# GpSimd's large work in the attention stage moves to VectorE and ScalarE

## The chip, the cores and the metric

The kernel runs on one core of one Trainium2 chip. The metric is device microseconds of one execution. The engines are TensorE (PE: matmuls and transposes; its weight loads are PEld), VectorE (DVE), ScalarE (ACT), GpSimd (POOL), and the DMA queue that SyncE (SP) issues.

## The reference

One step of a hybrid encoder layer, D_MODEL = 1024, 1024 new frames (prompt) and 32 frames of a running stream (sample, with 512 cached frames), 16 heads of 64. Both branches read one normed input `h`:

```python
q, k  = rmsnorm per head of h @ w_q, h @ w_k;  v = h @ w_v
logf  = log_sigmoid(h @ w_f + b_f)                 # forget gates, c = cumsum(logf)
u     = (h @ w_ua) * sigmoid(h @ w_ub)
s     = q k^T + c[t] - c[s], causal;  o = softmax(s) v
conv  = causal depthwise conv of u, width 31, + b_dw
ya    = (o * silu(h @ w_ga)) @ w_pa
yb    = (silu(layernorm(conv)) * silu(h @ w_gb)) @ w_pb
y     = x + (sigmoid(h @ w_ma) * ya + sigmoid(h @ w_mb) * yb) @ w_out
```

k, v, logf and the last 30 rows of u are outputs too, for both streams.

## The kernel before

All large products run on TensorE as three 16-bit products (high x high, high x low, low x high), so every operand is split into a high half (a rounded copy, on ScalarE) and a low half (value less high half, on VectorE or GpSimd). Weights come in blocks of 128 output columns. A `Batch` of two blocks loads them, takes their sum of squares on ScalarE (`stage`), totals it on PE (`total`), forms a power of two (`power`), and splits (`high`, `low`).

A projection of one block is 24 *beats*; a beat is three matmuls. `beat()` is the clock of the program's order: at each beat it runs what is due (`later(n, fn)` means n beats on) and, by a rate that each stage sets, takes instructions from `taps`. The order so made is kept for PE, VectorE, ScalarE (and SP in the attention stage).

`taps` is the list of VectorE's convolution steps. Per block f of 128 channels, `conv_taps(f)` appends 50 items: 46 multiply-adds of 128 x 543 (lines 402, 407, 411), 3 additions or subtractions (420 to 423), and a first item on ScalarE. `sums(f)` gives two more items for the LayerNorm's sums: `from_shift` (y less the mean over channels of block 0, line 359) and `into_sums` (line 366), each over pieces of 1024 and 32 columns; nine beats later ScalarE squares y, and four beats behind that GpSimd adds it into `rstd` (line 373). Block f's sums stand among the taps of block f+1; block 7's are run 28 beats after its last tap. After that `sides["ready"]` is set.

`u_tile(f)` opens the input block of a convolution; for f over 3 it first runs taps until at most 155 are left. At the end of the ga gates taps are run until at most 97 are left.

While the ga gates are projected (about 480 to 582 us), four `Sample` objects do the running stream's attention. `Sample.turn` (lines 1176 to 1182) transposes the softmax on PE in four full blocks and one of 32 rows. Both go to the one-bank PSUM pool "tr", each followed by a ScalarE copy out. The pool "st" has two banks.

The attention stage of the prompt (about 582 to 970 us) is a loop over 128 units, a unit being 128 queries of one head against 128 to 1024 keys. In each pair of heads the four query quarters come in the order 3, 1, 2, 0; a quarter holds two blocks of 128 queries, each for both heads (e = 0, 1). At step k the program issues:

- `scores` of unit k (PE, lines 1288 to 1290, into one of two banks pairs psS), `high` of unit k-3 (ScalarE, line 1318: the high half PH of P, the softmax)
- `top` and `soft` of unit k (VectorE's maximum, line 1297; ScalarE's exponential into P with its sum, line 1303)
- on even k the reciprocal of the sums, and the DMA transposes PH to PT (line 1335) of units k-5 and k-4
- what was put down for k: loads of the next pair, `values` (PE, line 1356, PT times V) eight units behind, `gated` (VectorE, line 1370)
- `low` of unit k-3, then taps as far as `slack` allows; one step of the LayerNorm generator `ln`, if `ready` is set and no bank is held.

P has four buffers and PH five; once `ready` is set, every third unit uses freed convolution tiles in place of these (`spare`). Between those steps come the *fills*: 22 blocks of the gb, ma and mb gates, 528 beats, spread over the units by the planner's cost per unit (`heavy`, `matmuls`).

`low` has two forms. For e = 0, and for all units once `taps` is empty, VectorE does it in one instruction (line 1327). For e = 1 while taps are left, GpSimd does it in two: P is scaled in place (line 1324), then PH's high half is subtracted (line 1325). The same condition governs the fill weights' high halves: while taps are left GpSimd makes them (line 154), and afterwards ScalarE (line 156). The planner's VectorE cost `vector(k)` counts `low` accordingly. The taps per unit follow from

```python
slack += R_A * (each * heavy(k) - vector(k) - 0.15 * share_of)     # R_A = 0.7
while taps and slack >= 0:
    slack -= 1.3 * (taps.pop(0)() or 1.0)                           # a tap returns 0.56, a sum nothing
```

Of the kernel before, what the change touches and what calls it, by code (L numbers as in the profile page):

```python
# [8 lines left out]
F32 = mybir.dt.float32  # L9
# [5 lines left out]
ALU = mybir.AluOpType  # L15
# [44 lines left out]
def build(tc, xT, xt, wv, wf, ckT, cv, clT, stT, vec, cst, yT, kT, vO, lfO, cpT, csT):  # L60
    nc = tc.nc
# [3 lines left out]
    def pool(name, bufs=1, stack=es, **kw):  # L65
        return stack.enter_context(tc.tile_pool(name=name, bufs=bufs, reuse_waits="tile", **kw))
# [27 lines left out]
    class Batch:  # L94
# [55 lines left out]
                                        op0=ALU.mult, op1=ALU.mult)  # L150

        def high(self, i, wh, raw, ks):
            if sides.get("cast") == "pool" and taps:
                nc.gpsimd.tensor_scalar(wh[:, ks, :], raw[:, ks, :], self.s[:, i:i + 1], 1.0, op0=ALU.mult, op1=ALU.mult)
                return
            nc.scalar.mul(wh[:, ks, :], raw[:, ks, :], self.s[:, i:i + 1])  # L156

        def low(self, i, wl, wh, raw, ks):
            nc.vector.scalar_tensor_tensor(wl[:, ks, :], raw[:, ks, :], self.s[:, i:i + 1], wh[:, ks, :],  # L159
                                           op0=ALU.mult, op1=ALU.subtract)  # L160
# [50 lines left out]
    def later(n, fn):  # L211

        pace["n"] += 1
        late.append((pace["tick"] + n, pace["n"], fn))
        late.sort(key=lambda e: e[:2])
# [89 lines left out]
    class Banks:  # L305

        n = 0
# [6 lines left out]
    st = pool("st", 2, stack=pps, space=PS)  # L314
    tr = pool("tr", 1, stack=pps, space=PS)
# [5 lines left out]
    taps = []  # L321
    pend = []

    def pump(n):
        for _ in range(min(n, len(taps))):
            taps.pop(0)()

    PCS = ((0, T, 0), (T + 30, TS, T))
    sides = {}

    def rounded(y):
        yr = cvp.tile([128, TT], F32R, name="shift", bufs=1)
        for o, n, a in PCS:
            nc.scalar.copy(yr[:, a:a + n], y[:, o:o + n])
# [17 lines left out]
    def kept(f, y):  # L352
        nc.sync.dma_start(s_y[f, :, :T], y[:, :T])
        nc.sync.dma_start(s_y[f, :, T:], y[:, T + 30:])

    def from_shift(f, y):
        shift = sides["shift"]
        for o, n, a in PCS:
            nc.vector.tensor_sub(y[:, o:o + n], y[:, o:o + n], shift[:, a:a + n])

    def into_sums(f, y):
        for o, n, a in PCS:
            if f == 0:
                nc.vector.tensor_copy(mean[:, a:a + n], y[:, o:o + n])
            else:
                nc.vector.tensor_add(mean[:, a:a + n], mean[:, a:a + n], y[:, o:o + n])

        def added():
            for o, n, a in PCS:
                if f == 0:  # L370
                    nc.gpsimd.tensor_copy(rstd[:, a:a + n], y[:, o:o + n])
                else:
                    nc.gpsimd.tensor_add(rstd[:, a:a + n], rstd[:, a:a + n], y[:, o:o + n])
            if f == 7:
                sides["ready"] = True

        later(9, lambda: nc.scalar.activation(y, y, AF.Square))
        later(13, added)

    def sums(f):  # L380
        return [lambda: from_shift(f, sides["y", f]), lambda: into_sums(f, sides["y", f])]

    def conv_taps(f):
        u = us.pop(f)

        w = lambda i: vec_t[:, V_WDW + f * KC + i:V_WDW + f * KC + i + 1]
        even, odd = u[:, 0:UW:2], u[:, 1:UW:2]
        V = nc.vector

        def ordered(t):  # L390
            if f > 5:
                tc.keep_in_program_order(t)
            return TAP

        def both(j):
            wj = wsum[:, f, j:j + 1]
            if j == 0:
                y = sides["y", f] = (u7p if f > 5 else cvp).tile([128, CW], F32, name="y", tag="y", bufs=2 if f > 5 else 3)
                nc.scalar.activation(y[:, 1:CW:2], odd[:, :CN], AF.Identity, bias=vcol(V_BDW, f), scale=wj)  # L399
                return 0.1  # L400
            y = sides["y", f][:, 1:CW:2]
            return ordered(V.scalar_tensor_tensor(y, odd[:, j:j + CN], wj, y, op0=ALU.mult, op1=ALU.add))  # L402

        def own(j):
            y = sides["y", f]
            e, o = y[:, 0:CW:2], y[:, 1:CW:2]
            return ordered(V.scalar_tensor_tensor(e, odd[:, j:j + CN], w(2 * j), e if j else o, op0=ALU.mult, op1=ALU.add))  # L407

        def other(j):
            o = sides["y", f][:, 1:CW:2]  # L410
            t = ordered(V.scalar_tensor_tensor(o, odd[:, j:j + CN], w(2 * j + 1), o, op0=ALU.mult, op1=ALU.add))  # L411
            if j == 14:
                kept(f, sides["y", f])
                if f == 7:
                    later(28, lambda: [fn() for fn in sums(7)])
            return t

        n = CN + 14
        items = [lambda j=j: both(j) for j in range(16)]
        items.append(lambda: ordered(V.tensor_sub(odd, even, odd)))  # L420
        items += [lambda j=j: own(j) for j in range(16)]
        items.append(lambda: ordered(V.tensor_sub(odd[:, :n], odd[:, :n], even[:, :n])))
        items.append(lambda: ordered(V.tensor_add(odd[:, :n], odd[:, :n], even[:, 1:1 + n])))
        items += [lambda j=j: other(j) for j in range(15)]
        if f < 6:
            taps.insert(max(0, len(taps) - 9), items.pop(0))
        if f == 7:
            taps.extend(items[:14] + pend + items[14:])
            pend.clear()
        else:  # L430
            taps.extend(items[:5] + pend + items[5:])
            pend[:] = sums(f) if f else []
# [5 lines left out]
        return ((slice(0, T - o), slice(30 + o, 30 + T)), (slice(T - o, n), slice(60 + T, 60 + T + TS)))  # L438

    def u_tile(f):  # L440
        if f > 3:
            pump(len(taps) - 155)
        u = us[f] = (u7p if f > 5 else cvp).tile([128, UW], F32, name="u", tag="u", bufs=2 if f > 5 else 4)
        nc.vector.memset(u[:, 0:30], 0.0)
        nc.sync.dma_start(u[:, 30 + T:60 + T], stT[f])
        return u
# [85 lines left out]
    def vcol(base, f):  # L532
        return vec_t[:, base + f:base + f + 1]
# [68 lines left out]
    def x_split(c, ws, u, jobs, ahead={}):  # L602
# [6 lines left out]
        def project(i, kt):  # L609
# [8 lines left out]
            if c == 2:  # L618
                for o2, n2, a2 in PCS:
                    b = slice(30 + o2, 30 + o2 + n2)  # L620
# [110 lines left out]
    for f in range(8):  # L731
# [15 lines left out]
    b2 = plan[0]  # L747
    x_split(0, ws0, u0, {
        0: [lambda: high(0, 0), lambda: low(0, 0), lambda: top(1), lambda: squares(2, False), lambda: low_pool(0, 1, True)],
        1: [lambda: squares(3), gains],  # L750
        2: [lambda: low_pool(0, 2, True), balance],
# [81 lines left out]
    for c in range(4):  # L833
# [16 lines left out]
        for t in range(8):  # L850
            ps = pj.tile([128, 512], F32, name="pjv", tag="pj")
            n = 0
            for kt in range(KT):
                sl = slice(t * 128, t * 128 + 128)
                wh, wl = wh2[kt // 4][:, kt % 4, :], wl2[kt // 4][:, kt % 4, :]
# [268 lines left out]
    class Sample:  # L1124
# [44 lines left out]
        def turn(self):  # L1169
            pf = self.pf  # L1170
            self.pts = pts = sp.tile([128, 7, 128], F32, name="pts", tag="kc", bufs=1)
            g = self.g
            nc.gpsimd.memset(pts[:, 4:7, :], 0.0)
            self.vn = pts[:, 5:7, :].rearrange("p a n -> p (a n)")
            nc.sync.dma_start(pts[:TS, 5:7, :], s_vs[:, 256 * g:256 * g + 256].rearrange("p (a n) -> p a n", a=2))
            pt = tr.tile([128, 512], F32, name="ptr2", tag="tr")
            for b in range(4):
                nc.tensor.transpose(pt[:, 128 * b:128 * b + 128], pf[:, 128 * b:128 * b + 128], ident)
            nc.scalar.copy(pts[:, 0:4, :], pt.rearrange("p (b q) -> p b q", b=4))
            pt = tr.tile([128, 512], F32, name="ptr2", tag="tr")  # L1180
            nc.tensor.transpose(pt[:TS, :128], pf[:, PAST:], ident)
            nc.scalar.copy(pts[:TS, 4, :], pt[:TS, :128])

# [59 lines left out]
    class Two:  # L1243
        n = 0
# [23 lines left out]
    class Unit:  # L1268
# [51 lines left out]
        def low(self):  # L1320
            n = self.i + 1
            f = self.f
            if self.e and taps:
                nc.gpsimd.tensor_scalar(self.P3, self.P3, f, 1.0, op0=ALU.mult, op1=ALU.mult)  # L1324
                nc.gpsimd.tensor_sub(self.H[:, :n, 1, :], self.P3, self.H[:, :n, 0, :])  # L1325
            else:
                nc.vector.scalar_tensor_tensor(self.H[:, :n, 1, :], self.P3, f, self.H[:, :n, 0, :],  # L1327
                                               op0=ALU.mult, op1=ALU.subtract)

        def turn(self):  # L1330
            i, e, m = self.i, self.e, self.i // 2
# [108 lines left out]
    width = lambda k: units[k].w if 0 <= k < len(units) else 0  # L1440
# [10 lines left out]

    def vector(k):

        return (0.31 + 0.00104 * width(k) + (0.1 + 0.001 * width(k - 3) if k % 2 or not taps else 0.0) +
                (0.5 if (k - 4 - LAG) % 4 == 0 else 0.0))

    BEAT = 0.447
# [9 lines left out]
    for g, p in enumerate(duos):  # L1467
# [9 lines left out]
        for n, m in enumerate(MORD):  # L1477
            k = t + 4 * n + 3 + LAG
# [65 lines left out]
    class Banks3:  # L1544
        n = 0
# [180 lines left out]
    parts = {}  # L1726
# [273 lines left out]
```

## Time and profile before

| | |
|---|---|
| median of 3 runs | 1252.08 us (1250.56 to 1255.34) |
| the profiled execution | 1253.4 us |
| its span, first to last instruction | 1251.5 us |
| mean granted TensorE clock | 0.995 |
| busy: PE, DVE, ACT, POOL | 1219.6, 1005.7, 791.8, 400.4 us |
| attention stage, taps present | about 582 to 724 us |
| attention stage, taps gone | about 724 to 970 us |

In the profile's windows each engine's busy time in the stretch is followed by its number of instructions, then come the granted TensorE clock, the share of DMA time and GB/s. A group's line reads: line, engine, operation, tiles written and read, shapes, count | busy us, mean ns of one | idle time before them and what ended it. A line of waits reads: who waited for whom, us in total, times, the longest. A line of the timeline reads: start, duration, engine, line, operation, and in brackets the idle time before it and what ended it.

### The profile page before, as it was taken

The page shows a single profiled execution, that of the slowest core. Times are in us where ns is not written, and L with a number is a line of the kernel's source. Part 1 is how long each engine was busy: PE and PEld are TensorE (multiplying, and loading weights), DVE is VectorE, ACT ScalarE, POOL GpSimd, SP SyncE. Part 2 cuts the span into 40 slices and gives each one's busy share as a digit, 9 for nine tenths or more (in the row PEclk, how much of TensorE's full clock was granted, in tenths as well). Part 3 has the DMA queues.
Part 4 walks back from the last instruction along what each step waited for, and adds up shares of the span by engine and source line. Part 5 has one row for each costly group of instructions (what it writes and reads, how often), then busy time and mean ns, then how long its engine had stood idle before and what let it go on. Part 6 is the DMA issues. An engine that isn't in the chain of part 4 may idle for free.

```text
span 1251.5 us, 24832 instructions
## 1 busy us (share of the span) xinstructions
PE 1219.6 (97%) x9288; PEld 852.1 (68%) x9288; DVE 1005.7 (80%) x1563; ACT 791.8 (63%) x1511; POOL 400.4 (32%) x443
## 2 busy tenths in 40 slices
PE   8999999999999999999899999999999999999998
PEld 5678786666666666666566656666666666666898
DVE  6799999988989999788999967887755586677764
ACT  5655554867768686446666777887866776644410
POOL 4046372637447271100565511000000000022652
PEclk9999999999999999999999999999999999999999
DMA  6335252332433246544999999999999885543561
GB/s 238 104 97 166 59 138 56 108 117 65 130 93 111 75 120 186 183 154 121 189 223 222 204 220 212 214 223 221 217 213 208 331 307 202 206 163 125 162 194 58
DMA packets 260840, 207.63 MB, mean 166 GB/s; under 512 B 187504, under 2 KB 223216, under 8 KB 260720
## 3 DMA queue, kind: packets, MB, share of 16 engines
q1 hardware_dynamic: 260576, 205.97, 61.1%
q8 instruction: 73, 1.20, 0.4%
q14 instruction: 47, 0.39, 0.1%
q10 hardware_dynamic: 144, 0.07, 0.0%
HBM read 110.97 MB, written 57.26 MB: 134 GB/s over the span
## 4 chain that ended last, share of the span: by engine, by line
PE 79%; DVE 6%; issue 5%; ACT 4%; POOL 4%; DMA 2%; SPq 0%; POOLq 0%; DVEq 0%; ACTq 0%
PE pj L201 56%; PE pjv L857 7%; PE pj L1830 6%; PE po L1356 3%; PE psS L1288 2%; PE psS L1289 1%; POOL PH L1325 1%; POOL P L1324 1%; DMA PT<-PH 1%; DVE y L402 1%; DVE wl L159 1%; ACT P L1303 1%; ACT PH L1318 1%; DVE nm L1297 1%; DVE PH L1327 1%
## 5 line engine op out<-in xcount | busy, mean ns | idle before, releaser
L201 PEld LDWEIGHTS <-wh 128*128 128x128 f16 x3840 | 376.0, 98 | 201.8 <-issue 2.4
L201 PE MATMUL pj<-xh,wh 128*128 128x352 f16 (+2 forms) x1536 | 481.1, 313 | 1.8 <-DVE qn L1003 1.6
L201 PE MATMUL pj<-xl,wh 128*128 128x352 f16 (+2 forms) x1536 | 480.5, 313 | 1.4 <-DVE xl L639 1.3
L201 PE MATMUL pj<-xh,wl 128*128 128x352 f16 (+2 forms) x1536 | 480.5, 313 | 0.1
L201 PEld LDWEIGHTS <-wl 128*128 128x128 f16 x1920 | 187.9, 98 | 90.5 <-issue 2.4
L159 DVE SCALAR_TENSOR_TENSOR wl<-raw,sc,wh 128x512 f16<-128x512 f32 (+1 forms) x158 | 131.9, 847 | 36.8 <-ACT wh L156 34.8
L1297 DVE TENSOR_REDUCE nm<-psS 128x1 f32<-128x1024 f32 (+7 forms) x128 | 96.4, 753 | 59.9 <-PE psS L1290 53.4
L1303 ACT ACTIVATE P<-psS,nm 128x1024 f32<-128x1024 f32 (+7 forms) x128 | 94.2, 736 | 63.5 <-DVE nm L1297 31.3
L402 DVE SCALAR_TENSOR_TENSOR y<-u,wsum,y 128x543 f32<-128x543 f32 x120 | 116.2, 968 | 4.8 <-ACT y L399 2.3
L149 POOL TENSOR_SCALAR sc<-sc,back 128x2 f32<-128x2 f32 (+1 forms) x37 | 25.9, 699 | 293.3 <-DVE sc L175 291.7
L407 DVE SCALAR_TENSOR_TENSOR y<-u,vec_t,y 128x543 f32<-128x543 f32 x128 | 115.1, 899 | 2.5
L411 DVE SCALAR_TENSOR_TENSOR y<-u,vec_t,y 128x543 f32<-128x543 f32 x120 | 108.0, 900 | 2.4
L1327 DVE SCALAR_TENSOR_TENSOR PH<-P,nm,PH 128x896 f16<-128x896 f32 (+7 forms) x106 | 91.1, 859 | 14.0 <-ACT PH L1318 12.9
L1318 ACT ACTIVATE PH<-P,nm 128x1024 f16<-128x1024 f32 (+7 forms) x128 | 98.4, 770 | 3.0 <-DMA PT<-PH 0.9
L156 ACT ACTIVATE wh<-raw,sc 128x1024 f16<-128x1024 f32 (+1 forms) x72 | 80.7, 1127 | 17.0 <-DVE sc L176 16.9
L121 ACT ACTIVATE junk<-raw 128x1024 bf16<-128x1024 f32 x78 | 81.8, 1049 | 0.2
L988 POOL TENSOR_TENSOR sql<-sqf,sqh 128x352 fp32r<-128x352 f32 x48 | 57.8, 1205 | 60.8 <-ACT sqh L985 60.7
L1288 PE MATMUL psS<-KB,QB 128*128 128x512 f16 (+2 forms) x192 | 63.3, 330 | 12.8 <-ACT P L1303 12.6
L857 PE MATMUL pjv<-vwh,xh 128*128 128x260 f16 x256 | 70.1, 274 | 0.0
L857 PE MATMUL pjv<-vwl,xh 128*128 128x260 f16 x256 | 70.0, 273 | 0.0
L857 PE MATMUL pjv<-vwh,xl 128*128 128x260 f16 x256 | 69.9, 273 | 0.0
L1356 PE MATMUL po<-PT,Vh 128*64 128x256 f16 (+1 forms) x640 | 56.3, 269 | 5.0 <-DMA PT<-PH 5.0
(318 smaller groups left out, 2372.1 us busy)
## 6 DMA issues: line engine op xcount, KB each, us to landing
raw<-wf SPq DMA_DIRECT2D x92, 512.0 KB
kT<-kun SPq DMA_DIRECT2D x8, 528.0 KB
s_ga<-t SPq DMA_DIRECT2D x24, 176.0 KB
s_gb<-t SPq DMA_DIRECT2D x24, 176.0 KB
s_ma<-t SPq DMA_DIRECT2D x24, 176.0 KB
s_mb<-t SPq DMA_DIRECT2D x24, 176.0 KB
wide<-s_o SPq DMA_DIRECT2D x8, 528.0 KB
wide<-s_y SPq DMA_DIRECT2D x8, 528.0 KB
```

The lines of the kernel that those rows point to most:

```text
L159: nc.vector.scalar_tensor_tensor(wl[:, ks, :], raw[:, ks, :], self.s[:, i:i + 1], wh[:, ks, :], op0=ALU.mult, op1=ALU.subtract)
L201: nc.tensor.matmul(ps, a[:, kt, :], b(kt, sl), start=(first and n == 0), stop=(last and n == N - 1))
L402: return ordered(V.scalar_tensor_tensor(y, odd[:, j:j + CN], wj, y, op0=ALU.mult, op1=ALU.add))
L407: return ordered(V.scalar_tensor_tensor(e, odd[:, j:j + CN], w(2 * j), e if j else o, op0=ALU.mult, op1=ALU.add))
L411: t = ordered(V.scalar_tensor_tensor(o, odd[:, j:j + CN], w(2 * j + 1), o, op0=ALU.mult, op1=ALU.add))
L857: nc.tensor.matmul(ps[:, :VC], a, b, start=(n == 0), stop=(n == 23))
L1288: nc.tensor.matmul(ps[:, ksl], QB[:, qsl], KB[:, ksl], start=True, stop=False)
L1297: nc.vector.tensor_reduce(self.nm[:, e:e + 1], self.ps[:, :self.w], axis=AX.X, op=ALU.max, negate=True)
L1303: nc.scalar.activation(self.P[:, :self.w], self.ps[:, :self.w], AF.Exp, bias=self.nm[:, e:e + 1], accum_out=self.nm[:, 2 + e:3 + e])
L1318: nc.scalar.mul(self.H[:, :n, 0, :], self.P3, self.f)
L1327: nc.vector.scalar_tensor_tensor(self.H[:, :n, 1, :], self.P3, f, self.H[:, :n, 0, :], op0=ALU.mult, op1=ALU.subtract)
L1356: nc.tensor.matmul(po[64 * e:64 * e + 64, 128 * ii.start:256], v[:, j, 64 * e:64 * e + 64], pt[:, ii, e, j, x, :], start=(j == 0 and n == ...
```

## The change

- The weights' high halves in the attention stage are always ScalarE's (the GpSimd branch in `high` is gone).
- P's low halves are always VectorE's, in one instruction (the GpSimd branch in `low` is gone); `vector(k)` counts it for every unit.
- The sums of blocks 6 and 7 are made in pieces of 344, 344 and 336 + 32 columns: six items in place of two. Block 7's are put down 28, 32, ... 48 beats after its last tap, in place of all at 28. The squaring and GpSimd's addition hang on the last piece.
- `u_tile` runs taps down to 155 for blocks 4 and 5 alone.
- The transpose of 32 rows in `Sample.turn` writes to a bank of "st" in place of "tr".

```diff
         def high(self, i, wh, raw, ks):
-            if sides.get("cast") == "pool" and taps:
-                nc.gpsimd.tensor_scalar(wh[:, ks, :], raw[:, ks, :], self.s[:, i:i + 1], 1.0, op0=ALU.mult, op1=ALU.mult)
-                return
             nc.scalar.mul(wh[:, ks, :], raw[:, ks, :], self.s[:, i:i + 1])
...
+    PC4 = ((0, 344, 0), (344, 344, 344), (688, 336, 688), PCS[1])
...
-    def into_sums(f, y):
-        for o, n, a in PCS:
+    def into_sums(f, y, pcs):
+        for o, n, a in pcs:
...
+        if pcs[-1] != PCS[-1]:
+            return
...
     def sums(f):
-        return [lambda: from_shift(f, sides["y", f]), lambda: into_sums(f, sides["y", f])]
+        parts = (PCS,) if f < 6 else ((PC4[0],), (PC4[1],), (PC4[2], PC4[3]))
+        return [lambda fn=fn, pcs=pcs: fn(f, sides["y", f], pcs) for pcs in parts for fn in (from_shift, into_sums)]
...
-                    later(28, lambda: [fn() for fn in sums(7)])
+                    for n, fn in enumerate(sums(7)):
+                        later(28 + 4 * n, fn)
...
     def u_tile(f):
-        if f > 3:
+        if 3 < f < 6:
             pump(len(taps) - 155)
...
-            pt = tr.tile([128, 512], F32, name="ptr2", tag="tr")
+            pt = st.tile([128, 512], F32, name="ptr2", tag="st")
             nc.tensor.transpose(pt[:TS, :128], pf[:, PAST:], ident)
...
         def low(self):
             n = self.i + 1
             f = self.f
-            if self.e and taps:
-                nc.gpsimd.tensor_scalar(self.P3, self.P3, f, 1.0, op0=ALU.mult, op1=ALU.mult)
-                nc.gpsimd.tensor_sub(self.H[:, :n, 1, :], self.P3, self.H[:, :n, 0, :])
-            else:
-                nc.vector.scalar_tensor_tensor(self.H[:, :n, 1, :], self.P3, f, self.H[:, :n, 0, :],
-                                               op0=ALU.mult, op1=ALU.subtract)
+            nc.vector.scalar_tensor_tensor(self.H[:, :n, 1, :], self.P3, f, self.H[:, :n, 0, :],
+                                           op0=ALU.mult, op1=ALU.subtract)
...
-        return (0.31 + 0.00104 * width(k) + (0.1 + 0.001 * width(k - 3) if k % 2 or not taps else 0.0) +
+        return (0.31 + 0.00104 * width(k) + 0.1 + 0.001 * width(k - 3) +
                 (0.5 if (k - 4 - LAG) % 4 == 0 else 0.0))
```

More of the change, by code (lines that the diff above doesn't have):

```diff
@@ L354, in kept, with from_shift @@
         nc.sync.dma_start(s_y[f, :, T:], y[:, T + 30:])
-    def from_shift(f, y):
+    def from_shift(f, y, pcs):
         shift = sides["shift"]
-        for o, n, a in PCS:
+        for o, n, a in pcs:
             nc.vector.tensor_sub(y[:, o:o + n], y[:, o:o + n], shift[:, a:a + n])
-    def into_sums(f, y):
-        for o, n, a in PCS:
+    def into_sums(f, y, pcs):
+        for o, n, a in pcs:
             if f == 0:
```

## The prediction

> **What bounds the kernel now.** I read the page's busy shares first, then the windows of the attention stage pair by pair, then the waits of its two parts, then the single rows behind the longest gaps.
>
> ```profile
> PE 1219.6 (97%) x9288; PEld 852.1 (68%) x9288; DVE 1005.7 (80%) x1563; ACT 791.8 (63%) x1511; POOL 400.4 (32%) x443
> ```
>
> TensorE is busy 97% of 1251.5 us. The change alters none of its work, so it can only take away its idle time or half-clock time. The next table has one row per pair of heads, 16 units each (the last is short); "taps" are the convolution steps on VectorE, the last of which runs at 722.8.
>
> ```profile
> core 0: us, PE busy (x) PEld busy (x) DVE busy (x) ACT busy (x) POOL busy (x), PEclk, DMA share, GB/s
> 582.00:630.00 48.00, 44.08 (x343) 28.83 (x341) 41.23 (x60) 35.75 (x76) 20.56 (x17) 1.00 0.84 188
> 630.00:678.00 48.00, 45.36 (x384) 30.36 (x383) 45.49 (x68) 31.80 (x72) 28.83 (x23) 1.00 1.03 219
> 678.00:728.00 50.00, 45.62 (x374) 30.15 (x373) 41.81 (x66) 33.94 (x78) 24.66 (x19) 0.97 0.96 213
> 728.00:774.00 46.00, 45.26 (x382) 30.20 (x380) 35.07 (x59) 36.51 (x82) 3.43 (x3) 1.00 0.95 212
> 774.00:821.00 47.00, 46.74 (x389) 31.81 (x387) 36.19 (x80) 38.18 (x84) 0.53 (x2) 1.00 1.01 220
> 821.00:867.00 46.00, 44.44 (x378) 29.72 (x376) 37.83 (x77) 38.14 (x88) 0.64 (x1) 1.00 1.05 222
> 867.00:916.00 49.00, 45.49 (x374) 30.57 (x371) 30.72 (x54) 37.06 (x80) 1.34 (x1) 0.97 1.00 212
> 916.00:960.00 44.00, 43.25 (x366) 28.98 (x366) 29.38 (x53) 34.49 (x74) 1.55 (x2) 1.00 1.02 219
> ```
>
> The first three pairs, with taps and with work on POOL, leave PE idle 3.92 + 2.64 + 4.38 = 10.94 us of 146. The other five, already without POOL work, leave 6.82 of 232. At their rate 146 us would hold 4.3. The waits say what ended the idle time, first of 582 to 728, then of 728 to 960 (us, times, longest):
>
> ```profile
> ACT P L1303 <- POOL PH L1325: 12.3, 7, 4.7
> ACT P L1303 <- DVE nm L1308: 11.3, 12, 2.3
> ACT P L1303 <- DVE nm L1297: 11.2, 8, 2.6
> PE psS L1288 <- ACT P L1303: 9.6, 8, 2.4
> PE po L1356 <- DMA PT<-PH: 1.2, 1, 1.2
> ```
> ```profile
> PE po L1356 <- DMA PT<-PH: 3.8, 3, 2.1
> PE psS L1288 <- ACT P L1303: 3.0, 5, 1.1
> ```
>
> In the first part PE waits for a score bank that the exponential P has not yet emptied (9.6 us), and a third of P's own idle time is POOL, which still holds P's buffer. In the second part that wait is 3.0 us in a stretch 1.6 times as long.
>
> **Term 1: P's low halves and the weights' high halves leave POOL.** What goes, of 582 to 728:
>
> ```profile
> L1325 POOL TENSOR_TENSOR PH<-P,PH 128x896 f16<-128x896 f32 (+7 forms) x22 | 33.7, 1530 | 1.7
> L1324 POOL TENSOR_SCALAR P<-P,nm 128x896 f32<-128x896 f32 (+7 forms) x22 | 25.9, 1175 | 51.3 <-ACT PH L1318 45.7 <-DMA KB<-s_k 4.2 <-DVE y L411 1.4
> L154 POOL TENSOR_SCALAR wh<-raw,sc 128x1024 f16<-128x1024 f32 x8 | 10.0, 1256 | 0.0
> ```
>
> That is 69.6 us of POOL. The longest PE gaps and what stood before them:
>
> ```profile
> 603.81 0.38 PE L1288 MATMUL psS<-KB,QB 128*128 128x512 f16 x1 [1.20 <-ACT P L1303]
> 622.03 0.22 PE L1288 MATMUL psS<-KB,QB 128*128 128x128 f16 x1 [0.73 <-ACT P L1303]
> 675.13 0.27 PE L1288 MATMUL psS<-KB,QB 128*128 128x256 f16 x1 [2.14 <-ACT P L1303]
> 723.97 0.27 PE L1288 MATMUL psS<-KB,QB 128*128 128x256 f16 x1 [2.38 <-ACT P L1303]
> ```
> ```profile
> 598.36 2.40 DVE L402 SCALAR_TENSOR_TENSOR y<-u,wsum,y 128x543 f32<-128x543 f32 x1
> 672.49 1.60 DVE L159 SCALAR_TENSOR_TENSOR wl<-raw,sc,wh 128x512 f16<-128x512 f32 x1 [1.02 <-POOL wh L154]
> 715.34 5.33 POOL L1324 TENSOR_SCALAR P<-P,nm 128x640 f32<-128x640 f32 x1 [3.86 <-ACT PH L1318]
> 620.77 1.05 POOL L1324 TENSOR_SCALAR P<-P,nm 128x640 f32<-128x640 f32 x1 [4.41 <-ACT PH L1318]
> ```
>
> Three of the gaps trace to POOL: at 603.81 a tap stretched to 2.40 us beside a POOL subtraction; at 675.13 VectorE waited for a weight half queued on POOL and then ran it slowly; at 723.97 one POOL scaling took 5.33 us where the same shape took 1.05, and P stood behind it. They are 1.20 + 2.14 + 2.38 = 5.7 us, and I take all of it as gained. The rest of the 9.6 (3.9) stays.
>
> Cost on VectorE: 22 lows at the mean of the second part, against the stretch that POOL's work gives VectorE today (the first three rows are 582 to 724, the next two the quiet 500 to 580, the last 728 to 960):
>
> ```profile
> L407 DVE SCALAR_TENSOR_TENSOR y<-u,vec_t,y 128x543 f32<-128x543 f32 x16 | 17.1, 1069 | 0.1
> L159 DVE SCALAR_TENSOR_TENSOR wl<-raw,sc,wh 128x512 f16<-128x512 f32 x16 | 16.5, 1042 | 1.1 <-POOL wh L154 1.0
> L402 DVE SCALAR_TENSOR_TENSOR y<-u,wsum,y 128x543 f32<-128x543 f32 x13 | 13.6, 1044 | 0.0
> ```
> ```profile
> L402 DVE SCALAR_TENSOR_TENSOR y<-u,wsum,y 128x543 f32<-128x543 f32 x15 | 11.8, 784 | 2.6 <-ACT y L399 2.3
> L159 DVE SCALAR_TENSOR_TENSOR wl<-raw,sc,wh 128x512 f16<-128x512 f32 x14 | 10.5, 748 | 5.0 <-ACT wh L156 5.0
> ```
> ```profile
> L1327 DVE SCALAR_TENSOR_TENSOR PH<-P,nm,PH 128x128 f16<-128x128 f32 (+7 forms) x80 | 67.1, 839 | 8.9 <-ACT PH L1318 8.7
> ```
>
> The lows add 22 x 0.84 = 18.5 us. The stretch comes back: 16 x 0.285 + 16 x 0.294 + 13 x 0.26 = 12.7 us. So VectorE gets about 6 us more, not 18.5. The Trainium skill (SBUF — State Buffer, "Who interferes with whom") says that a VectorE instruction with two SBUF inputs and a GpSimd instruction that reads SBUF exclude each other whole. The stretched rows on both sides agree with it, and by that rule alone the return would be larger than 12.7; the sum does not use it.
>
> On ScalarE eight high halves come in, 8 x about 1.15 us = 9 us in 146. It is busy 101 us there and 184 of 232 behind; that is the same share (75 against 79%) after the addition, so zero. Without that cover it would be part of the 9 us.
>
> On SP's queue, in order, transposes now stand behind VectorE's low instead of POOL's two passes, and later loads behind them gain; zero.
>
> **Term 2: the clock.**
>
> ```profile
> 724.80:728.20 3.40, 3.40 (x27) 2.05 (x22) 1.49 (x2) 1.98 (x6) 1.38 (x1) 0.50 1.45 214
> ```
>
> Behind the 2.38 us gap the granted clock is 0.50 for 3.4 us: half of that, 1.7 us, is lost, and goes with the gap. The 2.14 us gap at 675 cost none, so such a drop can also come back elsewhere.
>
> **Term 3: the small transpose of the running stream takes a bank of another pool.**
>
> ```profile
> L1181 PE MATMUL ptr<-ident,pf 128*32 128x128 f32 x4 | 1.1, 285 | 2.7 <-ACT pts L1179 2.7
> ```
>
> Four times PE waits until ScalarE has emptied the one bank, 2.7 us in all. The two "st" banks are free at that point (their last reader is `top`, 17 beats earlier), and PE is full around it: 2.7 gained, at worst 0.
>
> **Term 4: where the taps go.** Eight ga gates are 192 beats at 0.23, or 192 x 0.23 / 0.56 = 79 taps; attention starts with 48 items (44 taps, 3 differences and the sums of block 6 as two). So the list had 127 after block 7 put in 52, 93 just before its beats (48 x 0.21 / 0.56 = 18): never 155. The forced taps of blocks 6 and 7 do not exist, and leaving them out is worth 0; only the four added pieces make it 52.
>
> In attention the planner's mean unit is 2.78 us and 3.94 beats. Its free VectorE time per unit, at 0.7, was 0.78 us and becomes 0.54, since every low now counts. Items cost 46 x 0.728 + 2 x 1.3 = 36.1, then 46 x 0.728 + 6 x 1.3 = 41.3. So the taps end at unit 36.1 / 0.78 = 46 before (722.8 agrees) and 41.3 / 0.54 = 76 after, near 800. The same taps lie over 223 us instead of 146. VectorE there: 41.2 + 45.5 + 41.8 + 35.1 + 24 (31 of the next 47 us) = 188, plus 6, less some 5 of sums and LayerNorm that move behind: 189 of about 215, 88%, level, where it was 88% and then 77%. So units 46 to 76 get fuller. Price: the leftover 3.9 us per 146 held over 77 us is 2.1, against 3.0 / 232 x 77 = 1.0 there now: +1.1. Bounds: 0, and the full early rate 10.94 / 146 x 77 - 2.3 = +3.5. I take +1.1, as POOL's part of that rate is gone.
>
> Block 7's sums come in six pieces four beats apart, and the flag behind them 20 beats later.
>
> ```profile
> L562 DVE SCALAR_TENSOR_TENSOR rstd<-rstd,lt x6: 341/342/344, 819.6 to 859.7; 128x176 f32<-128x176 f32 x6
> ```
>
> Before, the flag rose near unit 58 (41 beats after the last tap) and LayerNorm's steps took until 859.7, unit 93: 36 units. After: 61 beats, 15 units, so unit 91, and 91 + 36 = 127 of 133. It just fits, cost 0; if some steps were left over they would run on VectorE in the bunch behind the last unit, 0.34 us an instruction under the remaining gate products: at most 2. The pieces of block 6 shorten the burst ahead of the 0.73 us gap at 622.03: -0.4.
>
> **Term 5: transposes.** When early pairs run at the later rate, they meet its waits for PT: 3.8 / 232 x 146 = 2.4 against 1.2 now, +1.2 (0 to +3).
>
> Sum: -5.7 - 1.7 - 2.7 + 1.1 - 0.4 + 1.2 = -8.2. The profiled execution took 1253.4 us (span 1251.5 and 1.9 around it), so 1245.2; it lies 1.3 above the median of the runs, 1252.1, so the forecast is 1244.
>
> **The rivals.**
> Cure complete: no price for terms 4 and 5, as in the windows from 728 to 821 (1.0 us idle in 93): -10.5, and some leftover gone too, 1240. Counted as the good end of the forecast.
> The waits only move: P's gaps go, but the bank waits turn into waits for PT (DMA share 0.84 to 1.05 in all eight windows, so it may already be near its limit) and into VectorE. Then only the transposes' 2.7 and about 1 us remain: 1248.5. Against it: pairs four and six took 46 us at the same DMA share.
> VectorE becomes the bound: the lows return, the taps stay for 30 units more, and VectorE in order delays each maximum. It decides if its share of units 0 to 76 passes the 88% of now. At the early rate for 223 us: 10.94 / 146 x 223 = 16.7 idle against 13.2 now, one more half-clock spell of 1.7, less 2.7: +2.5, 1255; with a quarter of the 18.5 us on PE's path as well, 1259. The Trainium skill speaks for it (Perfetto Trace Analysis, "Optimizing Scalar/DVE Operations"): with VectorE saturated, moving work off it, even to GpSimd, may pay, though the shared port may spoil that. The 5.33 us row shows the spoiling here, the 88% that VectorE was nearly saturated.
>
> **How the numbers follow.** Forecast 0.62 (1239 to 1248), waits move 0.23 (1246 to 1252), VectorE bound 0.15 (1253 to 1263). Half a per cent, about what a measurement here can tell from no change, is 6.3 us: faster is under 1245.8, slower over 1258.4. Of the forecast five sixths lie under: 0.53 faster; slower is half of the last rival, 0.08; the rest, 0.39, same. Range: below 1238 and above 1256 I leave out under 2 in 10.
>
> **What would show it.** Right: no POOL rows but the small scalings and the sums of squares from 582 on; taps near 0.78 us until about 800; the 0.50 clock at 725 gone; L1181 with no idle time; the three gaps gone; LayerNorm's last step near unit 127. Wrong: taps ending near 723, waits of psS for P that last past 728 at the early rate, or a sum of waits for PT well over 6 us.

## The result, and the profile after

The changed kernel takes 1244.09 us (median of 10 runs, 1240.01 to 1247.38) against 1253.08 of the kernel before (10 runs, 1249.91 to 1255.36). The ratio is 0.993, with a 95% interval of 0.9917 to 0.9943. The forecast was 1244 with a range of 1238 to 1256. The profiled execution took 1242.19 us and has a span of 1240.4. A run that lies over 1.5% above the fastest of its kernel is left out of the medians and ratios below (two runs of the last experiment).

The page's first lines after:

```profile
span 1240.4 us, 24761 instructions
PE 1216.3 (98%) x9288; PEld 851.2 (69%) x9288; DVE 1007.2 (81%) x1593; ACT 798.6 (64%) x1519; POOL 331.6 (27%) x391
```

GpSimd lost 69 us of work, VectorE gained 1.5 in spite of 22 more low halves, and PE's busy time fell by 3.3 us with the same 9288 matmuls. The last fits the clock: the trace of the kernel before has three spells of 3.4 us at half clock (from 21.6, 724.8 and 912.5 us), that of the changed kernel one (from 808.5), and two spells fewer are 3.4 us of matmul time. The windows of the attention stage again have one row per pair of heads, cut at each pair's first scores:

```profile
577.00:620.50 43.50, 43.50 (x342) 28.75 (x341) 35.91 (x60) 36.66 (x77) 0.27 (x1) 1.00 0.87 195
620.50:668.20 47.70, 44.93 (x380) 29.93 (x378) 36.98 (x66) 36.09 (x75) 4.86 (x4) 1.00 1.01 224
668.20:713.10 44.90, 44.42 (x376) 29.83 (x375) 40.79 (x72) 35.33 (x79) 0.27 (x1) 1.00 0.96 212
713.10:761.60 48.50, 44.63 (x375) 29.73 (x374) 38.47 (x66) 35.64 (x80) 0.27 (x1) 1.00 1.02 219
761.60:811.80 50.20, 46.34 (x377) 30.84 (x375) 38.51 (x67) 36.72 (x77) 0.53 (x2) 0.97 0.96 223
811.80:857.60 45.80, 44.23 (x375) 29.62 (x374) 36.41 (x64) 34.90 (x75) 4.21 (x3) 1.00 1.03 219
857.60:905.00 47.40, 47.40 (x394) 32.36 (x392) 35.65 (x76) 40.18 (x91) 1.36 (x1) 1.00 1.04 220
905.00:948.00 43.00, 42.25 (x349) 27.99 (x346) 34.15 (x70) 37.10 (x84) 0.77 (x2) 1.00 1.01 210
```

The first three pairs take 136.1 us in place of 146 and hold 3.25 us of PE idle time in place of 10.94. Pairs four and five take 98.7 in place of 93 and hold 7.7 in place of 1.0. So most of a first gain is given back. The same PE instruction, counted from the start in both traces, is 1.8 us earlier at 420 us (times of the changed kernel), 5.2 at the stage's beginning, 14.8 at 744, only 5.6 at 879, and 11.1 from 934 to the end. The 1.8 us at 420 come from the half-clock spell at 21.6 us, long before anything that the change touches: that part is luck. The last 5.5 come from waits for PT that the kernel before has behind 879 us, the longer one with the spell at 912.5; the changed kernel has none there. In the kernel before:

```profile
912.71 0.37 PE L1356 MATMUL po<-PT,Vh 128*64 128x256 f16 x1 [2.14 <-DMA PT<-PH]
```

The waits from 577 to 858 of the changed kernel:

```profile
ACT PH L1320 <- DMA PT<-PH: 22.9, 16, 4.1
PE po L1354 <- DMA PT<-PH: 7.3, 6, 3.5
PE psS L1290 <- ACT P L1305: 4.9, 4, 2.3
PEld L1354 <- DMA PT<-PH: 1.5, 2, 0.9
```

No wait for GpSimd is left. In its place ScalarE waits 22.9 us for PH buffers that a DMA transpose still reads (0.9 before, in the first part), and PE waits for PT. First what is left of the gap that stood at 675, then two such waits, on PE, with ScalarE's row behind the first of them:

```profile
665.77 0.27 PE L1290 MATMUL psS<-KB,QB 128*128 128x256 f16 x1 [1.00 <-ACT P L1305]
759.23 0.27 PE L1290 MATMUL psS<-KB,QB 128*128 128x256 f16 x1 [2.29 <-ACT P L1305]
754.90 0.93 ACT L1320 ACTIVATE PH<-P,nm 128x768 f16<-128x768 f32 x1 [4.06 <-DMA PT<-PH]
808.27 0.27 PE L1354 MATMUL po<-PT,Vh 128*64 128x256 f16 x1 [3.49 <-DMA PT<-PH]
808.50:811.97 3.47, 3.47 (x29) 2.41 (x25) 1.02 (x2) 2.11 (x5) 0.00 (x0) 0.51 1.01 249
```

The last row is a window: behind the 3.49 us gap the granted clock is 0.51 for 3.5 us, so a half-clock spell like the one that went at 725 has come back at 808.

### The profile page after: what moved, and what is told of

It is laid out like the page before. It is cut to its first block, busy times and chain, and to the rows that moved or that the text cites. A ratio compares the mean times of both kernels' runs of the same rounds, so it can differ in the third digit from the quotient of the medians.

```text
span 1240.4 us, 24761 instructions
## 1 busy us (share of the span) xinstructions
PE 1216.3 (98%) x9288; PEld 851.2 (69%) x9288; DVE 1007.2 (81%) x1593; ACT 798.6 (64%) x1519; POOL 331.6 (27%) x391
## 4 chain that ended last, share of the span: by engine, by line
PE 81%; DVE 6%; DMA 5%; ACT 4%; issue 2%; POOL 1%; SPq 0%; ACTq 0%; DVEq 0%; POOLq 0%
PE pj L198 58%; PE pjv L859 7%; PE pj L1828 6%; DMA PT<-PH 5%; PE po L1354 3%; PE psS L1290 2%; PE psS L1291 2%; DVE wl L156 1%; ACT PH L1320 1%; ACT P L1305 1%; DVE PH L1325 1%; DVE y L403 1%; ACT wh L153 1%; PE warm L527 1%; DVE nm L1299 1%
## 5 line engine op out<-in xcount | busy, mean ns | idle before, releaser
L156 DVE SCALAR_TENSOR_TENSOR wl<-raw,sc,wh 128x512 f16<-128x512 f32 (+1 forms) x158 | 125.5, 806 | 33.1 <-ACT wh L153 32.2
L1325 DVE SCALAR_TENSOR_TENSOR PH<-P,nm,PH 128x1024 f16<-128x1024 f32 (+7 forms) x128 | 107.8, 842 | 29.2 <-ACT PH L1320 27.9
L403 DVE SCALAR_TENSOR_TENSOR y<-u,wsum,y 128x543 f32<-128x543 f32 x120 | 113.1, 942 | 4.5 <-ACT y L400 2.0
L1320 ACT ACTIVATE PH<-P,nm 128x1024 f16<-128x1024 f32 (+7 forms) x128 | 98.4, 770 | 24.5 <-DMA PT<-PH 22.9
L408 DVE SCALAR_TENSOR_TENSOR y<-u,vec_t,y 128x543 f32<-128x543 f32 x128 | 110.4, 863 | 2.4
L412 DVE SCALAR_TENSOR_TENSOR y<-u,vec_t,y 128x543 f32<-128x543 f32 x120 | 108.7, 906 | 2.3
L153 ACT ACTIVATE wh<-raw,sc 128x1024 f16<-128x1024 f32 (+1 forms) x80 | 89.8, 1129 | 19.9 <-DVE sc L173 17.8
```

The lines of the kernel that those rows point to most:

```text
L1320: nc.scalar.mul(self.H[:, :n, 0, :], self.P3, self.f)
```

## The experiments

All ratios are to the kernel before on the same chip, with 95% intervals.

| kernel | median us | ratio | interval |
|---|---|---|---|
| the change | 1244.1 | 0.9930 | 0.9917 to 0.9943 |
| low halves alone | 1247.5 | 0.9964 | 0.9950 to 0.9978 |
| high halves alone | 1248.6 | 0.9971 | 0.9960 to 0.9982 |
| bank alone | 1246.9 | 0.9956 | 0.9944 to 0.9968 |
| change + GpSimd on scratch | 1261.7 | 1.0076 | 1.0062 to 1.0089 |
| change + 8 PH buffers | 1245.5 | 0.9943 | 0.9927 to 0.9958 |
| change, no store of y 7 | 1241.3 | 0.9919 | 0.9901 to 0.9937 |
| change, taps at 0.95 | 1242.1 | 0.9915 | 0.9902 to 0.9927 |
| change + 24 us on VectorE | 1246.1 | 0.9944 | 0.9929 to 0.9958 |
| change, stores on GpSimd's queue | 1238.2 | 0.9894 | 0.9876 to 0.9912 |
| change + 128 tiny loads on SP | 1267.1 | 1.0123 | 1.0108 to 1.0138 |
| stores moved and taps at 0.95 | 1237.1 | 0.9879 | 0.9865 to 0.9892 |
| and the heads' loads moved | 1256.0 | 1.0036 | 1.0011 to 1.0061 |

**The parts, each alone on the kernel before.** The first is `low` and `vector(k)` of the diff, the second `high`, the third the line with `st.tile`.

> The kernel before with one part of the change alone: P's low halves on VectorE for every unit, and the planner's cost that counts them (the weights' high halves stay on GpSimd, the bank and the sums as before). If GpSimd's low halves were what held P's buffers and stretched VectorE, this part brings 4 to 7 us (1246 to 1249). If the waits only move to VectorE or to the transposes, it brings 0 to 1 us (1252), and the gain of the whole came from the other parts.

Measured -4.5 us: the first theory. Aligned by PE instruction it is 9.1 us ahead at 738 us, only 1.5 at 885 and 5.8 from 934 on, so the giving back and the late gain belong to this part.

> The kernel before with the weights' high halves of the attention stage on ScalarE and nothing else. The gap of 2.14 us at 675 us stood behind a high half queued on GpSimd: 2 us gained (1250 to 1251) if such queueing is a cost of its own; 0 (1252 to 1253) if the low halves behind it on GpSimd set the pace anyway.

Measured -3.4 us: such queueing has a cost of its own, above the 2 expected. In the trace the gap of 2.14 us falls to 0.44; the rest comes from other gaps, above all that of 2.38 at 724, which falls to 1.11 and no longer has a half-clock spell behind it.

> The kernel before with the 32-row transpose in a bank of the other pool and nothing else. PE's four waits for ScalarE's copy (2.7 us) go: 1249 to 1250. If PE only waits elsewhere for the same copy, no change.

Measured -5.2 us (4.0 to 7.0). The four waits of 0.68 are gone:

```profile
L1183 PE MATMUL ptr<-ident,pf 128*32 128x128 f32 x4 | 1.1, 272 | 0.0
```

In the changed kernel's trace PE is ahead by 0.85 us after each of the four, 3.4 in all. In this kernel's own trace another 1.7 us are the spell at 21.6 us, which it lacks; the granted clock of its five runs (0.998 to 0.999, against a median of 0.997 in the 13 of the kernel before) fits that, but doesn't show which spells are missing in each run. So about 3.4 of the 5.2 are the change's, and the rest may be chance. The parts add up to 13.1 where the whole measured 9.0. Some of that is counted twice: the first two parts each take away the spell at 725 (1.7 us) and half or more of the gap before it.

The line in `u_tile` needs no run: built with and without it, the program is the same, so no tap was forced there. The sums' pieces were not run alone, so their share stays unmeasured.

**Does GpSimd cost by stretching VectorE, or by being waited for?**

```diff
+            if self.e and taps:      # y, z: scratch halves, x: the shift tile, read only
+                nc.gpsimd.tensor_scalar(y[:, :self.w], x[:, :self.w], 1.0, 1.0, op0=ALU.mult, op1=ALU.mult)
+                nc.gpsimd.tensor_sub(z[:, :self.w], x[:, :self.w], y[:, :self.w])
```

> The changed kernel with GpSimd doing two passes of the old shapes on scratch data beside VectorE's low halves of e = 1 while taps are left; nobody waits for them. If GpSimd's cost was that it stretches VectorE's instructions, much of the gain is lost: 1247 to 1251, with taps of about 1 us. If its cost was the wait for its results alone, the time stays at 1244 and only the durations on VectorE grow.

With nobody waiting, GpSimd ran its 36 pairs of passes (92 us) in one bunch beside the first two pairs of heads. From 577 to 688, this kernel first and the changed one second:

```profile
L156 DVE SCALAR_TENSOR_TENSOR wl<-raw,sc,wh 128x512 f16<-128x512 f32 x10 | 15.6, 1572 | 0.0
L403 DVE SCALAR_TENSOR_TENSOR y<-u,wsum,y 128x543 f32<-128x543 f32 x13 | 14.9, 1145 | 0.0
```
```profile
L403 DVE SCALAR_TENSOR_TENSOR y<-u,wsum,y 128x543 f32<-128x543 f32 x13 | 10.1, 778 | 0.0
L156 DVE SCALAR_TENSOR_TENSOR wl<-raw,sc,wh 128x512 f16<-128x512 f32 x12 | 8.8, 740 | 0.0
```

The first group takes 2.1 times as long, the second 1.5 times, and VectorE is busy 106 of the 111 us in place of 91. PE's waits for P are 13.3 us in that stretch, five half-clock spells follow them, and these two pairs take 110.1 us where the change takes 90.8. The loss, 17.6 us, is larger than the expected 3 to 7, since there were 36 pairs of passes in place of the 22 before, and they lay denser. So stretching alone is enough to cost once VectorE is nearly full; how the 22 pairs' own cost divides into stretching and waiting isn't separated by this run.

**Was VectorE the bound?**

```diff
+            if taps:      # y: a scratch tile of 128 x 176, x: the shift tile
+                nc.vector.scalar_tensor_tensor(y, x[:, :176], 1.0, x[:, 176:352], op0=ALU.mult, op1=ALU.subtract)
```

> The changed kernel with one more VectorE instruction of 0.34 us per unit while taps are left (76 of them, 26 us in all; it writes scratch that nobody reads). If VectorE is the bound there, most of the 26 us shows: 1260 or more. If it has room, 0 to 4 us: 1244 to 1248.

The trace has 73 of these instructions, 24.3 us in all, and VectorE is busy 200 of the 223 us from 577 to 800. The time rose by 2 us, with intervals that overlap. So VectorE still has room at this load, and the rival that it became the bound is out.

**What gives the gain back.** My first theory was the late flag, and with it the PH buffers.

```diff
-            self.H = (spare(self, "y", F16, [128, 8, 2, 128]) or
-                      ap.tile([128, 8, 2, 128], F16, name="PH", tag="PH", bufs=PHB))
+            m = 8 if n > 4 else 4
+            self.H = ap.tile([128, m, 2, 128], F16, name="PH", tag=f"PH{m}", bufs=4)
...
+            self.P = ap.tile([128, T], F32, name="P", tag="P", bufs=4)      # no spare
...
+    sides["shift"] = u7p.tile([128, TT], F32, name="shift", tag="u", bufs=2)
```

> The changed kernel with eight PH buffers from the start of the attention stage, four of 8 key blocks and four of 4, in place of five (and no spare ones later; the shift tile stands in a convolution buffer). In the changed kernel ScalarE's high half waits 23 us for a PH buffer that a transpose still reads, once 4.1 us with PE idle behind it. If the flag that brings spare buffers, now about 30 units later, is what gives gain back between units 46 and 91, these waits go and the time is 1238 to 1241. If the transposes are late because DMA is at its limit, PE then waits at PT in place of P and the time stays at 1243 to 1245.

The theory fell: 1245.5. ScalarE's wait for PH is gone from the waits between 577 and 858, and PE's wait for PT grew:

```profile
PE po L1354 <- DMA PT<-PH: 9.9, 8, 3.0
PE psS L1290 <- ACT P L1305: 1.9, 2, 1.5
```

The buffers were where the lateness showed, not what caused it: the transposes are late.

```diff
-                kept(f, sides["y", f])
+                if f < 7: kept(f, sides["y", f])      # and s_y[6] is read for s_y[7]
```

> The changed kernel without the store of block 7's convolution output (0.5 MB, issued at unit 79 right ahead of the transposes; block 6's is read in its place). If that store is what makes PE wait 3.5 us for PT at unit 80, with the half-clock spell behind it, 3 to 5 us are gained (1239 to 1241). If the buffers alone make it late, the wait stays and the time is 1243 to 1245.

The wait at unit 80 fell from 3.49 to 2.20 us and the spell behind it went. The time, -2.8, points the same way, but its interval overlaps the change's: the store is a part of it at most.

```diff
-R_U, R_V, R_QK, R_G, R_A = 0.21, 0.18, 0.165, 0.23, 0.7
+R_U, R_V, R_QK, R_G, R_A = 0.21, 0.18, 0.165, 0.23, 0.95
```

> The changed kernel with the taps taken at 0.95 of the planner's free VectorE time in place of 0.7: they end near unit 56 in place of 75, and the flag rises near unit 72 in place of 91. If the late flag costs, this gains 1 to 3 us (1241 to 1243). If VectorE is the bound while the taps last, the fuller queue loses 2 to 6 us (1246 to 1250).

-2.0, with intervals that just overlap: inconclusive alone, and against the rival that a fuller VectorE loses.

The second theory: SP issues transposes, loads and stores in one order, and its queue is nearly full. From 577 to 960 its rows cover 350 of 383 us, though a transpose's row also holds SP's own waiting (1.17 us at the least, 1.93 on average). Around the wait at unit 80, first VectorE's low half of unit 71, whose PT PE waits for there, then SP of the changed kernel:

```profile
792.65 0.75 DVE L1325 SCALAR_TENSOR_TENSOR PH<-P,nm,PH 128x512 f16<-128x512 f32 x1
799.83 0.47 SPq L1102 DMA_DIRECT2D KA<-s_k  x1
800.36 0.35 SPq L113 DMA_DIRECT2D raw<-wf  x1
800.75 0.42 SPq L1344 DMA_DIRECT2D ga<-s_ga  x1
801.27 0.38 SPq L1083 DMA_DIRECT2D s_ma<-t  x1
801.75 0.38 SPq L351 DMA_DIRECT2D s_y<-y  x1
802.18 0.47 SPq L352 DMA_DIRECT2D s_y<-y  x1
802.70 4.85 SPq L1333 DMA_TRANSPOSE PT<-PH  x2
```

The low half is done at 793.4, and SP begins to issue its transpose 9.3 us later. Two other transposes and ten other DMAs stand between; the last six of these take SP 2.9 us.

```diff
-            stored(lambda: nc.sync.dma_start(s_g[g][f, :, sl], t))
+            stored(lambda: (nc.gpsimd if sides.get("queue") else nc.sync).dma_start(s_g[g][f, :, sl], t))
```

> The changed kernel with the gates' 66 stores of the attention stage issued from GpSimd's DMA queue, now idle, in place of SP's. With eight PH buffers ScalarE's waits went and PE waited at PT instead, so the transposes themselves are late. If they are late because SP issues them in order behind some 0.4 us for each store (SP would be about nine tenths full with 1.9 us for each transpose), this takes 26 us off SP and most of the 7 us of waits for PT: 1238 to 1241. If DMA's own work is the limit, the stores cost the same from another queue: 1243 to 1246.

1238.2, wholly below the change's interval. The bytes are the same; from 577 to 858 the wait for PT falls from 7.3 to 2.6:

```profile
PE po L1354 <- DMA PT<-PH: 2.6, 3, 1.5
PEld L1354 <- DMA PT<-PH: 1.4, 2, 0.8
```

SP's rows still cover 349 of 383 us, but now SP waits more for VectorE's low halves. From 577 to 960, the changed kernel first and this one second:

```profile
SPq L1333 <- DVE PH L1325: 31.6, 27, 2.8
SPq L1333 <- DVE PH L1325: 67.5, 32, 4.6
```

The mean time from the end of a low half to the end of its transpose's issue falls from 6.7 to 5.5 us. (A store also makes SP wait for ScalarE's tile, 16.7 us in all in the changed kernel; the gain holds both.)

```diff
         if u:
             u.scores()
+            nc.sync.dma_start(tiny()[0:1, :], s_m[0:1, 0:8])
```

> The changed kernel with one more load of 32 bytes per unit on SP's queue (128 of them, some 0.4 us of SP each, nothing to move). If SP's issuing in order is the limit, the transposes come 0.4 us later at each unit and 5 to 20 us are lost (1249 to 1264). If DMA's data or packets are the limit, nothing is seen: 1243 to 1246.

1267.1, 23 us slower than the change with 4 kB more moved. The loads' own rows, and PE's wait from 577 to 960:

```profile
L1499 SPq DMA_DIRECT2D tiny<-s_m x128: 215/280/837, 577.0 to 976.7; - x128
PE po L1354 <- DMA PT<-PH: 25.3, 12, 5.5
```

128 issues of 0.28 us (median) are about 36 us of SP, and PE's wait for PT grows by 18. From a low half's end to the end of its transpose's issue it now takes 8.9 us on average. PE's matmul still follows 1.4 to 4.0 us behind the end of the issue at each of its waits over a microsecond; in the change it is 2.0 to 3.4 at the four waits over 0.6. So it is the issuing order on SP, not data.

**A version that beats both kernels.** Stores on GpSimd's queue and taps at 0.95:

> The gates' stores on GpSimd's queue and the taps at 0.95 of the free VectorE time together: the latter alone took 2 us off. If both causes are real and apart, 1236 to 1239; if the stores' queue is of no account, 1241 to 1243 as with the taps alone.

1237.1, ratio 0.9879, as expected if the two are apart. But the interval overlaps that of the stores alone (0.9876 to 0.9912), so the second gain isn't shown by the time. The wait for PT is nearly gone (577 to 960), and the mean time from low half to issued transpose is 4.9 us:

```profile
PE po L1354 <- DMA PT<-PH: 0.9, 2, 0.7
```

```diff
-            nc.sync.dma_start(dst, src)
+            (nc.gpsimd if sides.get("queue") else nc.sync).dma_start(dst, src)      # and Vh, Vl alike
```

> The last one with the heads' loads (Q, K and V of the next pair, ten a pair) on GpSimd's queue too, so that SP holds little but transposes. If SP still orders the transposes late, another 1 to 3 us are gained (1234 to 1236). If the 0.9 us of waits for PT that were left there was all there is to gain, it stays at 1236 to 1238; if GpSimd's queue becomes the late one, it loses (1239 or more).

1256.0, 19 us slower than the last. Waits from 577 to 970, then the time to landing of loads and of transposes (577 to 960):

```profile
PE po L1354 <- DMA PT<-PH: 15.2, 6, 5.2
POOL s_gb L1083 <- DMA QA<-s_q: 8.8, 2, 5.0
KB<-s_k POOLq DMA_DIRECT2D x12, 256.0 KB, 8.1
PT<-PH SPq DMA_TRANSPOSE x125, 5.6
```

GpSimd's queue then holds stores up behind loads (8.8 us), and its loads take 5.5 to 8.9 us to land. The transposes, alone on SP but for a few, are issued sooner than in any other run: 3.5 us after the low half on average. They land later: in PE's six waits the matmul starts 5.5 to 11.4 us after the end of its transpose's issue, where the change has 2.0 to 3.4. So here the transfers are slow, not the order; what slows them is not shown.

## Why the prediction was right, and where its steps were not

- **Bound and place.** Right: only PE's idle and half-clock time moved, and the gain came in the first three pairs. That it moved behind them too is the step below that failed.
- **Term 1 (-5.7).** Right in mechanism, under-sized: idle fell by 7.7 us in those pairs. The three gaps gave 4.7 of their 5.7 (that at 675 keeps 1.00), and the "rest" that was to stay went as well: 1.56 us at 716, 0.73 at 622 and 0.76 at 628, for instance. That VectorE would not be charged the full 18.5 us is right: quiet taps of 778 to 780 ns. Its load there fell from 128.5 to 113.7 us, also because fewer taps fall there now. The forecast of 88%, level, was too high: units 0 to 76 measure 83% (184.0 of 220.6 us).
- **Term 2 (-1.7).** The spell at 725 went, one came at 808, the one at 912 went: net the 1.7 that were forecast, but by other spells, so the agreement is luck. That one could come back elsewhere was said.
- **Term 3 (-2.7).** Right in sign; 3.4 in the trace.
- **Term 4.** The taps ended at 797 (near 800 foretold), LayerNorm at 944.7, near unit 126 (127 foretold), and the forced taps were none. The price of 1.1 for a fuller VectorE was for a cause that hardly costs: 24 us more of it cost 2. The -0.4 for the pieces of block 6 was not measured alone.
- **Term 5 (+1.2) and "on SP's queue ... zero".** This is the step that failed. With GpSimd out of the way SP's order became the next bound, and pairs four and five lost 6.7 us to PE's idle time, not the 2.3 that terms 4 and 5 had, besides the spell at 808. One of the prediction's own signs of being wrong, waits for PT well over 6 us, came near: 7.3 us, and 1.5 more of weight loads. I had seen the transposes move from behind GpSimd to behind VectorE, and had not added up what SP issues in one pair.
- **The sum.** -8.2 foretold, -9.0 measured. It came out by errors of both signs. In the two traces, 11.1 us apart, 1.8 are the spell at 21.6 us, 3.4 term 3, 9.6 the gain up to 744 us (7.8 foretold in terms 1, 2 and the -0.4), -9.2 what was given back up to 879 (-2.3 foretold), and 5.5 the late waits that went, which no term had. So a number this close is partly luck. The late gain stands in the trace of the low halves alone as well (4.3 us); why those waits went is open. The rival "the waits only move" was half of the truth.

## What to carry to other kernels

When an engine that others wait for is relieved, add up the next queue in order before pricing it at zero: here 128 transposes and some 190 other DMAs on one queue, where 0.28 us more a unit cost 23 us and 66 stores fewer gained 6. A full buffer pool is a symptom until more buffers help; ask who frees them. In this kernel GpSimd's passes were paid for on VectorE too, so weigh such an offload by VectorE's durations with and without it.

## What the runs showed of the hardware that was not expected

- The first half-clock spell (at 21 to 25 us, granted 0.51) stands in the trace of the kernel before and not in the bank's, though PE's order is the same in both there: about 1.7 us of chance from one profiled execution to another. The length of a gap alone didn't decide on a spell: in the kernel before gaps of 2.38 us (at 724) and 2.14 (at 912) had one, and a gap of 2.14 at 675, like one of 2.29 at 759 in the changed kernel, had none.
- GpSimd's passes, when they lie close, made VectorE's instructions 1.5 to 2.1 times as long in the groups shown (778 to 1145 and 740 to 1572 ns).
- What SP pays for a DMA hardly follows its size: 0.28 us (median) for a load of 32 bytes; in the rows at 800 us 0.47 for 12 KB (KA) and 0.35 for 512 KB (raw, a weight block).
